# A planned float32 decoder layer: engine prices taken from the trace, the gates' strip loaded early, the residual stored by SyncE

## The chip, the cores and the metric

The kernel runs on one core of one Trainium2 chip. The metric is device microseconds of one execution. Engines: TensorE (PE), VectorE (DVE), ScalarE (ACT), GpSimd (POOL), and SyncE (SP), which only issues DMAs. ScalarE issues DMAs too, on a queue of its own; both queues are served by the core's 16 DMA engines.

## The reference, cut to what matters

One decoder layer for 256 tokens of 2048 features, all in float32:

```
sh1, sc1, g1, ..., g3 = split(silu(c) @ ada_w + ada_b, 9)
h = h + 0.5 * g1 * swiglu(modulate(rms_norm(h), sh1, sc1), ffn1 weights)
u = modulate(rms_norm(h), sh2, sc2)
p = u @ w_in            # q,k,v,z of DeltaNet; beta and decay gates (32 columns); q,k,v of attention; two merge gates
y_a = gated_delta_chunked(...)      # 16 heads, chunks of 64 tokens
y_b = moba_attention(...)           # 16 heads, causal, with a relative-position bias
h = h + g2 * ((sigmoid(gate_a) * (y_a @ w_proj_a) + sigmoid(gate_b) * (y_b @ w_proj_b)) @ w_out)
h = h + 0.5 * g3 * swiglu(modulate(rms_norm(h), sh3, sc3), ffn2 weights)
```

## The kernel before, in words

**Weights.** The dense products are cut into units, and a unit into steps of 128 rows (one k-tile) by 1024 columns of weights, 512 KB. A step's raw weights come by one or two DMAs on SyncE's queue into a ring of eight slots (`load_w`, L392 on; `fill`, `one_load`). `split` makes two fp32r parts of them: ScalarE casts to `wh`, VectorE subtracts to get `wl`. It runs LEAD = 3 steps ahead of TensorE, and VectorE's end of `wl` frees the ring slot. A step is then twelve matmuls of 512 columns (`mm`, L465): two token tiles, two column halves, three products (wh by the high part of x, wl by the high part, wh by the low part). There are 912 steps.

**Side work.** Everything else (norms, transposes, the DeltaNet and attention heads, the adaLN sections) is written as generators. `aside` puts one into a list with the time at which it can go on; `pump`, called once or twice a step, lets a generator run to its next `yield` if it is ready and if VectorE and ScalarE have room before the next weights are due. All of this happens while the program is written, so it fixes each engine's order of instructions. The times are those of `Clock`, an account that adds a price to an engine for every instruction issued through the wrappers V, S, PE, G (L184 is the wrapper's call, so all side work has this line). A generator is ready when what its last piece wrote is ready by the account (`clk.turn`), or at a time that it yields, such as `clk.PE + 8.0`. `late`, up to which side work may fill VectorE and ScalarE, counts the steps split ahead at W_STEP = 12 * W_MM each. `Clock.add` prices a DMA at 0.06 us of its engine plus DMA_LAG until it has landed.

**The mixer.** It follows the first FFN. `begin` in `mixer()` takes the residual `h` (eight pages of 128x512) out of use. At the mixer's step 8 (`KT // 2`) the hook `spill` stores all eight pages to DRAM (`hsp`) from ScalarE's queue and starts two generators, in this order:
- `late_params` loads the convolution weights and more, after 8 us zeroes two scratch arrays in DRAM (`xsc`, four stores of 256 KB), loads the tables of the position bias, and after 12 us stores the bias spread over 128 rows for each of 16 heads, 3 MB (`scr`), all from ScalarE's queue.
- `heads_params` loads the 128-column strip of w_in that holds the beta and decay gates, in two halves of 512 KB (rows of 512 bytes), from SyncE's queue (L956), each into a ring slot; 8 us after a half's issue ScalarE and VectorE split it in two parts. Then come 48 matmuls (16 k-tiles, three products each), the gates' arithmetic on small tiles, and a store of the cumulated decays (`gsc`).

Each DeltaNet group (four heads) later goes through DRAM several times: `dn_tile` loads a row of `gsc` and stores the matrix L to `lsc`; `dn_blocks` loads its diagonal blocks, inverts them, stores them into `xsc` and loads the whole matrices back (four loads of 256 KB) for TensorE. `dn_front` and `dn_back` use GpSimd's power. The units of the merge gates and the projections begin after `need_dn` and `need_mb`, which let all groups end. `reload_h` reads `hsp` back later.

Tiles of 128x512 come from a pool of 57 pages. `pump` holds a generator back when too few are free.

Of the kernel before, what the change touches and what calls it, by code (L numbers as in the profile page):

```python
# [13 lines left out]
F32 = mybir.dt.float32  # L14
# [29 lines left out]
OPEN = 8  # L44
FINISH = 3
BLOCKS = ((0, 4), (4, 8), (8, 12), (12, 16))
W_MM = 0.216
W_STEP = 12 * W_MM
W_H = 1.0
W_L = 1.2  # L50
RESERVE = 1.0
DMA_LAG = 2.6
AHEAD_LAST = 4.0
SPARE = 10
SPARE_ON = 3
HEADS_ON = 2
MB = 6
MB_MIX = 5
MARGIN = 0.0

CON = {}
_n = 0
# [48 lines left out]
    __slots__ = ("unit", "kt", "cols", "x", "first", "last", "load", "wh", "wl", "xs", "ready")  # L111


class Clock:

    def __init__(self):
        self.PE = self.ACT = self.DVE = self.POOL = 0.0
        self.after = self.turn = 0.0  # L120
        self.count = 0
        self.wrote, self.read = {}, {}
        self.spent = {"PE": 0.0, "ACT": 0.0, "DVE": 0.0, "POOL": 0.0}

    def begin(self):

# [2 lines left out]

    def seen(self, log, name, eng):  # L130
        t, by = log.get(name, (0.0, eng))
        return t + (0.05 if by == eng else 0.18)

    def free(self, name, eng):
        return max(self.seen(self.wrote, name, eng), self.seen(self.read, name, eng))
# [6 lines left out]
    def add(self, eng, op, args, kw):  # L142
        self.count += 1
        aps = [(k, a) for k, a in (*enumerate(args), *kw.items()) if isinstance(a, bass.AP)]
        outs = [a.tensor.name for k, a in aps if k in (0, "out", "accum_out")]
        ins = [a.tensor.name for k, a in aps if k not in (0, "out", "accum_out")]
        out = args[0] if args else kw["out"]
        n = 1
        for d in out.shape[1:]:
            n *= d  # L150
        lag = 0.0
        if op == "dma_start":
            cost, lag = 0.06, DMA_LAG
        elif eng == "PE":
            cost = 0.003 + n / 2400 * (1 if args[2].dtype == F32R else 2 if op == "transpose" else 4)
        elif eng == "DVE":
            cost = 0.065 + n / (960 if op in ("tensor_tensor", "tensor_sub", "tensor_add", "tensor_mul", "scalar_tensor_tensor") else 1500)
            if any(x.startswith("bk") for x in ins):
                cost = max(cost, 0.065 + n / 960) + 0.06
        elif eng == "ACT":  # L160
            cost = 0.1 + n / 1200
        else:
            cost = 0.9 + n / 30 if op == "tensor_tensor" else 0.1 + n / 290
        start = max([getattr(self, eng)] + [self.seen(self.wrote, x, eng) for x in ins] + [self.free(x, eng) for x in outs])
        end = start + cost
        setattr(self, eng, end)
        self.spent[eng] += cost
        for x in ins:
            self.read[x] = (end + lag, eng)
        for x in outs:  # L170
            self.wrote[x] = (end + lag, eng)
        self.after = end + lag + 0.18
        self.turn = max(self.turn, self.after)


# [22 lines left out]
def tile_hybrid_layer(ctx: ExitStack, tc: tile.TileContext, A, out, dbg=None):  # L198
# [5 lines left out]
    ctx.enter_context(tc.manual_schedule())  # L204

    clk = Clock()
    V, S, PE, G = (Timed(e, clk, n) for e, n in ((nc.vector, "DVE"), (nc.scalar, "ACT"), (nc.tensor, "PE"), (nc.gpsimd, "POOL")))
    serial = [0]
    held = []
    taken = [0]  # L210
# [60 lines left out]
    def ring_tile(shape):  # L271
        ring["out"] += 1
        return sb.tile(list(shape), F32, name=nm("ring"), tag="ring", bufs=RING)

    def ring_done():
        ring["out"] -= 1
# [212 lines left out]
    def aside(gen):  # L489
        side.append(Side(gen, clk.turn))  # L490
# [457 lines left out]

    def heads_params():

        parts = []
        for half in range(2):
            while ring["out"] >= RING:
                yield
            raw = ring_tile((P, 8, P))
            nc.sync.dma_start(raw, W_IN[half * 8 * P:(half + 1) * 8 * P, oB:oB + P].rearrange("(k p) n -> p k n", p=P))  # L956
            yield clk.PE + 8.0
            for n in range(2):
                wh, wl = page((P, 4, P), F32R), page((P, 4, P), F32R)
                S.copy(wh, raw[:, n * 4:n * 4 + 4, :])  # L960
                V.tensor_sub(wl, raw[:, n * 4:n * 4 + 4, :], wh.bitcast(F32))
                parts.append((wh, wl))
                if n:
                    ring_done()
                yield
        uh, ul = state["u"]
        b = sbank()
        for kt in range(KT):
            wh, wl = (w[:, kt % 4, :] for w in parts[kt // 4])
            PE.matmul(b[:, :T], wh, uh[:, kt, :], start=kt == 0, stop=False)  # L970
            PE.matmul(b[:, :T], wh, ul[:, kt, :], start=False, stop=False)
            PE.matmul(b[:, :T], wl, uh[:, kt, :], start=False, stop=kt == KT - 1)
        parts = None
        ba = page((2 * HEADS, T))
        V.tensor_copy(ba, b[:2 * HEADS, :T])
        yield
        b = sbank()
        for tt in range(NT):
            PE.transpose(b[:, tt * 32:tt * 32 + 32], ba[:, tt * P:(tt + 1) * P], ident[:32, :32])
        ab = small(64, "ab")  # L980
        V.tensor_copy(ab, b[:, :64])
        ab3 = ab.rearrange("p (t n) -> p t n", t=NT)
        W = NT * HEADS
        be = const(W, "beta")
        be3 = be.rearrange("p (t n) -> p t n", t=NT)
        S.activation(be3, ab3[:, :, 0:HEADS], AF.Tanh, scale=0.5)
        V.tensor_scalar(be, be, 0.5, 0.5, op0=ALU.mult, op1=ALU.add)
        yield
        x = small(W, "x")
        V.tensor_tensor(x.rearrange("p (t n) -> p t n", t=NT), ab3[:, :, HEADS:], dtb[:, None, :].to_broadcast([P, NT, HEADS]), op=ALU.add)  # L990
        e = small(W, "e")
        S.activation(e, x, AF.Abs)
        S.activation(e, e, AF.Exp, scale=-1.0)
        al = small(HEADS, "al")
        S.activation(al, alog, AF.Exp)
        yield
        z = small(W, "z")
        V.tensor_scalar(z, e, 2.0, None, op0=ALU.add)
        V.reciprocal(z, z)
        V.tensor_mul(z, z, e)  # L1000
        z2 = small(W, "z2")
        V.tensor_mul(z2, z, z)
        acc = small(W, "lp")
        V.tensor_scalar(acc, z2, 1.0 / 17, None, op0=ALU.mult)
        for k in range(7, 0, -1):
            V.scalar_tensor_tensor(acc, acc, 1.0 / (2 * k + 1), z2, op0=ALU.add, op1=ALU.mult)
        V.scalar_tensor_tensor(acc, acc, 1.0, z, op0=ALU.add, op1=ALU.mult)
        V.tensor_scalar(x, x, 0.0, None, op0=ALU.max)
        V.scalar_tensor_tensor(acc, acc, 2.0, x, op0=ALU.mult, op1=ALU.add)
        g = const(W, "g")  # L1010
        V.scalar_tensor_tensor(g.rearrange("p (t n) -> p t n", t=NT), acc.rearrange("p (t n) -> p t n", t=NT), -1.0,
                               al[:, None, :].to_broadcast([P, NT, HEADS]), op0=ALU.mult, op1=ALU.mult)
        yield
        b = sbank()
        for n, m in enumerate((C("tri"), bc(C("one0"), [P, P]), bc(C("one1"), [P, P]))):
            PE.matmul(b[:, n * W:(n + 1) * W], m, g, start=True, stop=True)
        gc = const(W, "gc")
        V.tensor_copy(gc, b[:, 0:W])
        ngc = const(W, "ngc")
        V.tensor_scalar(ngc, gc, -1.0, None, op0=ALU.mult)  # L1020
        rem = const(W, "rem")
        for n in range(2):
            r0 = n * 64
            V.tensor_sub(rem[r0:r0 + 64, :], b[r0:r0 + 64, (n + 1) * W:(n + 2) * W], gc[r0:r0 + 64, :])
        S.activation(rem, rem, AF.Exp)
        tot = const(2 * W, "tot")
        S.activation(tot, b[:, W:3 * W], AF.Exp)
        beg = const(W, "beg")
        S.activation(beg, gc, AF.Exp)
        V.tensor_mul(beg, beg, be)  # L1030
        beh = const(W, "beh")
        V.tensor_scalar(beh, be, 0.5, None, op0=ALU.mult)
        yield
        b = sbank()
        PE.transpose(b[:W, :P], gc, ident)
        gr = page((W, P))
        S.copy(gr, b[:W, :P])
        yield
        S.dma_start(gsc, gr)
        dn.update(be=be, beh=beh, gc=gc, ngc=ngc, rem=rem, tot=tot, beg=beg)  # L1040
# [516 lines left out]
    def mixer():  # L1557
        def begin():
            set_banks(MB_MIX)
            grow.pop(1)  # L1560
            held.clear()
            h, state["h"] = state["h"], None

            def spill():
                for tt in range(NT):
                    for n in range(4):
                        S.dma_start(hsp[:, tt, n * 512:(n + 1) * 512], h[tt][n])
                clk.turn = clk.PE
                aside(late_params())
                aside(heads_params())  # L1570
            hooks.setdefault(mix_at[0] + KT // 2, []).append(spill)

        mix_at = [nsteps[0]]
        ks = list(range(KT))
# [179 lines left out]
```

## Time and profile before, and how to read it

| | us |
|---|---|
| median of 3 runs | 2821.92 (2816.88 to 2828.46) |
| the profiled execution | 2811.26 |
| its span, first to last instruction | 2809.5 |
| mean granted TensorE clock | 0.995 of full speed |

The profile is of one execution. An engine's busy time is the union of its instructions. "a <- b" after an idle time names what ended the wait; a wait's list has total us, times, longest us. PEld is the weight load of TensorE. pg is any page, bk any PSUM bank.

### The profile page before, as it was taken

Reading aid. Unit: us, or ns where it says so; the run is one execution under the profiler, and the core shown is the slowest. Engines: PE = TensorE matmul, PEld = TensorE weight load, DVE = VectorE, ACT = ScalarE, POOL = GpSimd, SP = SyncE. Lnnn points to the kernel's source line nnn. Section 1 sums busy time; section 2 is a strip of 40 time slices with the busy share of each in tenths; the row PEclk is TensorE's granted clock in tenths of the full one; section 3 lists DMA queues with packets and bytes.
Section 4 is the critical chain, followed back from the end, with each engine's and each line's share of the span. In section 5 each row is a group of like instructions: output and inputs, shape, how many; then the busy total and the mean of one; then the engine's idle time right before and its main releaser. Section 6 shows DMA issues by size and latency. Waiting matters only on the chain.

```text
span 2809.5 us, 36472 instructions
## 1 busy us (share of the span) xinstructions
PE 2726.4 (97%) x12696; PEld 2256.8 (80%) x12696; DVE 2008.2 (71%) x2778; ACT 1386.9 (49%) x2166; POOL 47.1 (2%) x43
## 2 busy tenths in 40 slices
PE   5999999999998999999999999999999999999999
PEld 3888888888876888788888888888878888888887
DVE  6699788797954676867666899889656666544545
ACT  5534453444463564554645655455564444443443
POOL 0000000000000000000100000000000000000000
PEclk9999999999999999999999999999999999999999
DMA  9898659898968664646555998989557777656654
GB/s 333 278 314 280 215 184 358 278 354 303 337 204 204 188 180 138 175 124 171 159 156 164 317 284 283 327 300 337 185 160 240 245 241 247 210 190 194 194 187 135
DMA packets 321190, 658.34 MB, mean 234 GB/s; under 512 B 44815, under 2 KB 67938, under 8 KB 321006
## 3 DMA queue, kind: packets, MB, share of 16 engines
q1 hardware_dynamic: 282432, 634.97, 69.2%
q10 hardware_dynamic: 38574, 21.05, 3.2%
q8 instruction: 99, 1.62, 0.2%
q14 instruction: 85, 0.70, 0.1%
HBM read 644.86 MB, written 11.03 MB: 233 GB/s over the span
## 4 chain that ended last, share of the span: by engine, by line
PE 87%; DMA 5%; DVE 3%; ACT 3%; issue 1%; ACTq 0%; POOL 0%; SPq 0%; DVEq 0%; POOLq 0%
PE bk L465 81%; PE bk L184 6%; DMA ring<-in_w_in 2%; DVE pg L184 2%; ACT pg L184 1%; DVE wl L184 1%; DMA pg<-xsc 1%; ACT wh L184 1%; DMA ring<-in_ada_w 0%; ACT uh L184 0%; DMA pg<-in_x 0%; ACTq L184 0%; DMA xsc<-pg 0%; DMA ring<-in_w_proj_a 0%; DMA lsc<-pg 0%
## 5 line engine op out<-in xcount | busy, mean ns | idle before, releaser
L184 DVE TENSOR_TENSOR wl<-ring,wh 128x1024 fp32r<-128x1024 f32 x912 | 1112.9, 1223 | 597.7 <-ACT wh L184 583.4
L184 ACT CAST wh<-ring 128x1024 fp32r<-128x1024 f32 x912 | 959.9, 1055 | 972.6 <-PE bk L465 794.4
L465 PE MATMUL bk<-wh,uh 128*128 128x512 f32 x2560 | 1022.6, 399 | 3.4 <-ACT uh L184 2.6
L465 PE MATMUL bk<-wl,uh 128*128 128x512 f32 x2560 | 1001.3, 391 | 0.9 <-DVE wl L184 0.8
L465 PE MATMUL bk<-wh,ul 128*128 128x512 f32 x2560 | 853.5, 391 | 2.6 <-DVE ul L184 2.6
L465 PE MATMUL bk<-wh,pg 128*128 128x512 f32 x2176 | 719.1, 390 | 4.0 <-DVE pg L184 3.5
L465 PEld LDWEIGHTS bk<-wh,ul 128*128 128x128 f32 x2560 | 482.1, 188 | 109.4 <-DVE ul L184 6.3
L465 PEld LDWEIGHTS bk<-wh,uh 128*128 128x128 f32 x2560 | 483.1, 189 | 99.4 <-ACT uh L184 4.2
L465 PEld LDWEIGHTS bk<-wl,uh 128*128 128x128 f32 x2560 | 483.5, 189 | 94.9 <-DVE wl L184 2.2
L465 PEld LDWEIGHTS bk<-wh,pg 128*128 128x128 f32 x2176 | 408.5, 188 | 91.5 <-DVE pg L184 5.4
L465 PE MATMUL bk<-wl,pg 128*128 128x512 f32 x1088 | 423.6, 389 | 0.0
L184 DVE SCALAR_TENSOR_TENSOR pg<-ring,csil,pg 128x512 f32<-128x512 f32 x552 | 388.5, 746 | 8.2 <-DMA ring<-in_ada_w 8.2
L465 PEld LDWEIGHTS bk<-wl,pg 128*128 128x128 f32 x1088 | 204.3, 188 | 42.2
L184 ACT COPY pg<-bk 128x512 f32<-128x512 f32 (+3 forms) x201 | 108.6, 563 | 183.7 <-PE bk L184 108.5
L184 DVE TENSOR_TENSOR pg<-bk,pg 128x512 f32<-128x512 f32 (+3 forms) x225 | 148.6, 677 | 46.4 <-PE bk L465 38.4
L184 DVE TENSOR_TENSOR pg<-pg,pg 128x256 fp32r<-128x256 f32 (+11 forms) x388 | 159.3, 415 | 6.0 <-ACT pg L184 0.9
L184 PE MATMUL bk<-con,pg 128*128 128x128 f32 (+2 forms) x775 | 118.4, 277 | 42.2 <-DVE pg L184 17.4
L184 PEld LDWEIGHTS bk<-con,pg 128*128 128x128 f32 (+2 forms) x775 | 95.8, 142 | 68.4 <-DVE pg L184 17.1
L184 PEld LDWEIGHTS bk<-pg,pg 128*128 128x128 f32 (+2 forms) x834 | 111.3, 192 | 26.3 <-issue 15.2
L184 PE MATMUL bk<-pg,pg 128*128 128x128 f32 (+3 forms) x834 | 118.7, 287 | 12.5 <-DMA pg<-xsc 10.3
L184 ACT ACTIVATE pg<-pg 128x128 f32<-128x128 f32 (+1 forms) x176 | 78.6, 451 | 50.9 <-DVE pg L184 29.1
L184 ACT ACTIVATE pg<-bk 128x128 f32<-128x128 f32 (+1 forms) x136 | 60.0, 451 | 78.9 <-PE bk L465 45.0
(110 smaller groups left out, 679.3 us busy)
## 6 DMA issues: line engine op xcount, KB each, us to landing
ring<-in_ffn_w SPq DMA_DIRECT2D x704, 256.0 KB, 4.1
ring<-in_ada_w SPq DMA_DIRECT2D x288, 512.0 KB, 5.4
ring<-in_w_in SPq DMA_DIRECT2D x512, 256.0 KB, 4.2
ring<-in_ffn_w SPq DMA_DIRECT2D x176, 512.0 KB, 4.6
ring<-in_w_in SPq DMA_DIRECT2D x34, 512.0 KB, 4.7
ring<-in_w_proj_a SPq DMA_DIRECT2D x64, 256.0 KB, 5.2
ring<-in_w_proj_b SPq DMA_DIRECT2D x64, 256.0 KB, 5.9
ring<-in_w_out SPq DMA_DIRECT2D x32, 512.0 KB, 4.3
```

The costliest lines, as they stand in the source:

```text
L184: r = f(*args, **kw)
L465: nc.tensor.matmul(st.unit.banks[tt, c], xs[i == 2][:, tt * P:(tt + 1) * P], w[:, c * 512:(c + 1) * 512], start=st.first and i == 0, stop= ...
```

## The change

Three edits.

- The account's prices and rules are replaced: the matmul of 512 columns from 0.216 to 0.2268 us, DMA issue from 0.06 to 0.4, DMA landing from 2.6 to 5.0, GpSimd's power from 0.9 + n/30 to 0.35 + 0.17 n, extra price for per-partition scalar operands, for accumulating outputs and for reductions, semaphore delays between engines from 0.18 to 0.13 or 0.2 us; a generator must now be ready 0.3 us (MARGIN) before TensorE's time. SyncE gets a wrapper, SY.
- `heads_params` issues the strip as four loads of 256 KB into four pages at mixer step 4, waits 32 us (HEADS_WAIT) on the account's clock, then splits the four parts as before.
- The eight pages of the residual are stored from SyncE's queue, one at each of the mixer's steps 4 to 11; `late_params` starts at step 9.

```diff
-W_MM = 0.216
+W_MM = 0.2268
-DMA_LAG = 2.6
+DMA_LAG = 5.0
+DMA_ISSUE = 0.4
-MARGIN = 0.0
+MARGIN = 0.3
+HEADS_WAIT = 32.0
...
     def seen(self, log, name, eng):
         t, by = log.get(name, (0.0, eng))
-        return t + (0.05 if by == eng else 0.18)
+        return t + ((0.0 if eng == "PE" else 0.05) if by == eng else 0.2 if by == "PE" else 0.13)
...
+        ps = any(x.startswith("bk") for x in ins)
+        each = sum(size(a) == 1 for k, a in aps if k not in (0, "out", "accum_out")) if n > 1 else 0
         lag = 0.0
         if op == "dma_start":
-            cost, lag = 0.06, DMA_LAG
+            cost, lag = DMA_ISSUE, DMA_LAG
         elif eng == "PE":
-            cost = 0.003 + n / 2400 * (1 if args[2].dtype == F32R else 2 if op == "transpose" else 4)
+            cost = 0.003 + n / 2400 * 2 if op == "transpose" else 0.0135 + n / 2400 if args[2].dtype == F32R else 0.008 + n / 2400 * 4
         elif eng == "DVE":
-            cost = 0.065 + n / (960 if op in ("tensor_tensor", "tensor_sub", "tensor_add", "tensor_mul", "scalar_tensor_tensor") else 1500)
-            if any(x.startswith("bk") for x in ins):
-                cost = max(cost, 0.065 + n / 960) + 0.06
+            if op == "tensor_reduce":
+                n = size(args[1])
+            two = op in ("tensor_tensor", "tensor_sub", "tensor_add", "tensor_mul", "scalar_tensor_tensor", "tensor_reduce")
+            cost = 0.068 + 0.06 * each + n / (960 if two or ps else 1900)
         elif eng == "ACT":
-            cost = 0.1 + n / 1200
+            cost = (0.055 if ps else 0.1) + 0.09 * (each + ("accum_out" in kw)) + n / 1200
         else:
-            cost = 0.9 + n / 30 if op == "tensor_tensor" else 0.1 + n / 290
-        start = max([getattr(self, eng)] + [self.seen(self.wrote, x, eng) for x in ins] + [self.free(x, eng) for x in outs])
+            cost = 0.35 + 0.17 * n if op == "tensor_tensor" else 0.12 + n / 1000
+        start = max([getattr(self, eng)] + [self.seen(self.wrote, x, eng) for x in ins]
+                    + [self.seen(self.read, x, eng) if op == "dma_start" else self.free(x, eng) for x in outs])
...
-        self.after = end + lag + 0.18
+        self.after = end + lag + 0.2
...
     def heads_params():
 
+        raws = [page((P, 4, P)) for _ in range(4)]
+        for n in range(4):
+            SY.dma_start(raws[n], W_IN[n * 4 * P:(n + 1) * 4 * P, oB:oB + P].rearrange("(k p) n -> p k n", p=P))
+        yield clk.PE + HEADS_WAIT
         parts = []
-        for half in range(2):
-            while ring["out"] >= RING:
-                yield
-            raw = ring_tile((P, 8, P))
-            nc.sync.dma_start(raw, W_IN[half * 8 * P:(half + 1) * 8 * P, oB:oB + P].rearrange("(k p) n -> p k n", p=P))
-            yield clk.PE + 8.0
-            for n in range(2):
-                wh, wl = page((P, 4, P), F32R), page((P, 4, P), F32R)
-                S.copy(wh, raw[:, n * 4:n * 4 + 4, :])
-                V.tensor_sub(wl, raw[:, n * 4:n * 4 + 4, :], wh.bitcast(F32))
-                parts.append((wh, wl))
-                if n:
-                    ring_done()
-                yield
+        for n in range(4):
+            wh, wl = page((P, 4, P), F32R), page((P, 4, P), F32R)
+            S.copy(wh, raws[n])
+            V.tensor_sub(wl, raws[n], wh.bitcast(F32))
+            parts.append((wh, wl))
+            raws[n] = None
+            yield
...
-            def spill():
-                for tt in range(NT):
-                    for n in range(4):
-                        S.dma_start(hsp[:, tt, n * 512:(n + 1) * 512], h[tt][n])
-                clk.turn = clk.PE
-                aside(late_params())
-                aside(heads_params())
-            hooks.setdefault(mix_at[0] + KT // 2, []).append(spill)
+            def spill(n):
+                SY.dma_start(hsp[:, n // 4, n % 4 * 512:(n % 4 + 1) * 512], h[n // 4][n % 4])
+                h[n // 4][n % 4] = None
+            for n in range(8):
+                hooks.setdefault(mix_at[0] + 4 + n, []).append(lambda n=n: spill(n))
+
+            def params(gen):
+                clk.turn = clk.PE
+                aside(gen())
+            for n, gen in ((4, heads_params), (KT // 2 + 1, late_params)):
+                hooks.setdefault(mix_at[0] + n, []).append(lambda gen=gen: params(gen))
```

## Rows read from the trace of the kernel before

**Rows 1.** The page: span, TensorE's busy time, the DMA packets.
```profile
span 2809.5 us, 36472 instructions
...
PE 2726.4 (97%) x12696; PEld 2256.8 (80%) x12696; DVE 2008.2 (71%) x2778; ACT 1386.9 (49%) x2166; POOL 47.1 (2%) x43
...
DMA packets 321190, 658.34 MB, mean 234 GB/s; under 512 B 44815, under 2 KB 67938, under 8 KB 321006
```
**Rows 2.** Windows: us, busy time (instructions) of each engine, clock, DMA share, GB/s.
```profile
0.00:100.00 100.00, 65.30 (x272) 52.74 (x273) 69.26 (x96) 52.81 (x88) 1.65 (x7) 1.00 0.94 331
...
1000.00:1600.00 600.00, 582.64 (x3064) 490.74 (x3063) 425.70 (x806) 327.94 (x717) 34.32 (x19) 0.99 0.60 172
```
**Rows 3.** Waits of TensorE, 780 to 912 us: total, times, longest.
```profile
PE bk L184 <- ACT pg L184: 13.3, 2, 11.2
...
PE bk L465 <- DVE wl L184: 0.8, 1, 0.8
PE bk L465 <- ACT wh L184: 0.6, 1, 0.6
```
**Rows 4.** Waits of TensorE, 912 to 2060 us.
```profile
PE bk L184 <- DMA pg<-xsc: 10.3, 6, 2.7
PE bk L184 <- DVE pg L184: 6.3, 7, 1.6
PE bk L465 <- DVE pg L184: 3.5, 4, 1.9
```
**Rows 5.** Timeline, 857 to 886 us: start us, us, engine, instruction [idle before].
```profile
857.92 0.67 ACTq L184 DMA_DIRECT2D scr<-pg  x1
...
858.58 0.38 SPq L956 DMA_DIRECT2D ring<-in_w_in  x1
...
884.44 0.62 ACT L184 CAST pg<-ring 128x512 fp32r<-128x512 f32 x1 [19.10 <-DMA ring<-in_w_in]
...
885.12 0.58 PE L184 MATMUL bk<-uh,pg 128*128 128x256 f32 x1 [11.24 <-ACT pg L184]
```
**Rows 6.** DMA queues, 862 to 884 us: packets, MB, share of 16 engines.
```profile
q10 hardware_dynamic: 1422, 2.18, 87.1%
q1 hardware_dynamic: 1287, 0.99, 13.4%
```
**Rows 7.** Windows of two stretches at half clock.
```profile
877.44:891.09 13.65, 5.97 (x25) 5.70 (x26) 3.81 (x5) 3.03 (x4) 0.00 (x0) 0.50 1.00 191
1082.24:1085.65 3.41, 3.41 (x12) 2.93 (x12) 2.20 (x3) 0.00 (x0) 0.00 (x0) 0.50 0.00 1
```
**Rows 8.** Timeline at the spill.
```profile
814.99 0.40 ACTq L184 DMA_DIRECT2D hsp<-pg  x1
...
825.23 1.99 ACT L184 CAST wh<-ring 128x1024 fp32r<-128x1024 f32 x2 [5.46 <-DMA hsp<-pg]
```
**Rows 9.** SyncE's own waits, 770 to 910 us.
```profile
SPq L402 <- DVE wl L184: 54.9, 23, 10.8
```
**Rows 10.** The chain of waits: start us, us, what.
```profile
129.06 81.64 PE bk L465 x360
```
**Rows 11.** DMA issues: count, KB each, median us to landing.
```profile
pg<-xsc ACTq DMA_DIRECT2D x16, 256.0 KB, 5.8
```
**Rows 12.** Timeline, a DeltaNet group's loads and TensorE's wait for them.
```profile
1071.70 2.07 ACTq L184 DMA_DIRECT2D pg<-xsc  x4
...
1081.78 1.63 PE L184 MATMUL bk<-pg,pg 128*128 128x128 f32 x8 [2.09 <-DMA pg<-xsc]
```
**Rows 13.** Groups of instructions by form: busy us, mean ns, then idle before.
```profile
L184 DVE SCALAR_TENSOR_TENSOR pg<-ring,csil,pg 128x512 f32<-128x512 f32 x552 | 388.5, 746 | 8.2 <-DMA ring<-in_ada_w 8.2
...
L184 POOL TENSOR_TENSOR rkq<-ssq,mhalf 128x16 f32<-128x16 f32 x4 | 12.6, 3142 | 424.7 <-DVE ssq L184 412.9 <-DVE st L184 11.8
```
**Rows 14.** Two tiles' instructions: duration ns min/median/max, first and last start us.
```profile
L184 DVE SCALAR_TENSOR_TENSOR pg<-pg,sa,pg x32: 343/347/353, 1135.5 to 1503.2; 128x128 f32<-128x128 f32 x32
...
L402 SPq DMA_DIRECT2D ring<-in_w_proj_a x64: 328/424/1053, 1580.9 to 1770.1; - x64
```

More of the change, by code (lines that the diff above doesn't have):

```diff
@@ L111, with size @@
     __slots__ = ("unit", "kt", "cols", "x", "first", "last", "load", "wh", "wl", "xs", "ready")
+def size(ap):
+    n = 1
+    for d in ap.shape[1:]:
+        n *= d
+    return n
 class Clock:
     def __init__(self):
-        self.PE = self.ACT = self.DVE = self.POOL = 0.0
+        self.PE = self.ACT = self.DVE = self.POOL = self.SP = 0.0
         self.after = self.turn = 0.0
@@ L122, in __init__ @@
         self.wrote, self.read = {}, {}
-        self.spent = {"PE": 0.0, "ACT": 0.0, "DVE": 0.0, "POOL": 0.0}
+        self.spent = {"PE": 0.0, "ACT": 0.0, "DVE": 0.0, "POOL": 0.0, "SP": 0.0}
     def begin(self):
@@ L147, in add @@
         out = args[0] if args else kw["out"]
-        n = 1
-        for d in out.shape[1:]:
-            n *= d
+        n = size(out)
+        ps = any(x.startswith("bk") for x in ins)
+        each = sum(size(a) == 1 for k, a in aps if k not in (0, "out", "accum_out")) if n > 1 else 0
         lag = 0.0
         if op == "dma_start":
-            cost, lag = 0.06, DMA_LAG
+            cost, lag = DMA_ISSUE, DMA_LAG
         elif eng == "PE":
-            cost = 0.003 + n / 2400 * (1 if args[2].dtype == F32R else 2 if op == "transpose" else 4)
+            cost = 0.003 + n / 2400 * 2 if op == "transpose" else 0.0135 + n / 2400 if args[2].dtype == F32R else 0.008 + n / 2400 * 4
         elif eng == "DVE":
-            cost = 0.065 + n / (960 if op in ("tensor_tensor", "tensor_sub", "tensor_add", "tensor_mul", "scalar_tensor_tensor") else 1500)
-            if any(x.startswith("bk") for x in ins):
-                cost = max(cost, 0.065 + n / 960) + 0.06
+            if op == "tensor_reduce":
+                n = size(args[1])
+            two = op in ("tensor_tensor", "tensor_sub", "tensor_add", "tensor_mul", "scalar_tensor_tensor", "tensor_reduce")
+            cost = 0.068 + 0.06 * each + n / (960 if two or ps else 1900)
         elif eng == "ACT":
-            cost = 0.1 + n / 1200
+            cost = (0.055 if ps else 0.1) + 0.09 * (each + ("accum_out" in kw)) + n / 1200
         else:
-            cost = 0.9 + n / 30 if op == "tensor_tensor" else 0.1 + n / 290
-        start = max([getattr(self, eng)] + [self.seen(self.wrote, x, eng) for x in ins] + [self.free(x, eng) for x in outs])
+            cost = 0.35 + 0.17 * n if op == "tensor_tensor" else 0.12 + n / 1000
+        start = max([getattr(self, eng)] + [self.seen(self.wrote, x, eng) for x in ins]
+                    + [self.seen(self.read, x, eng) if op == "dma_start" else self.free(x, eng) for x in outs])
         end = start + cost
@@ L206, in tile_hybrid_layer @@
     clk = Clock()
-    V, S, PE, G = (Timed(e, clk, n) for e, n in ((nc.vector, "DVE"), (nc.scalar, "ACT"), (nc.tensor, "PE"), (nc.gpsimd, "POOL")))
+    V, S, PE, G, SY = (Timed(e, clk, n) for e, n in ((nc.vector, "DVE"), (nc.scalar, "ACT"), (nc.tensor, "PE"), (nc.gpsimd, "POOL"), (nc.sync, "SP")))
     serial = [0]
```

## The prediction

> **What bounds the kernel now.** I read the page first. TensorE is busy 97% of the span, 2726.4 of 2809.5 us [rows 1], and its work isn't changed: every matmul and transpose stands in both versions. So the change can only act on the 83.1 us in which TensorE is idle, and on what a slowed TensorE clock costs. The windows then say where the idle time lies: 34.7 us of it in the first 100 us [rows 2], which no edit reaches, since the opening is issued in a fixed order. Of the rest I asked the waits of TensorE, stretch by stretch. Between 60 and 780 us the list is empty. From 780 to 912 us one wait stands out, 11.2 us on ScalarE [rows 3]. From 912 to 2060 us there are seventeen short ones, 20.1 us in all, none over 2.7 us [rows 4]. After that come only the hand-written passage into the last FFN and the final stores, both as they were.
>
> The timeline shows what the long wait is. The store of the attention's bias table (scr, 3 MB) is issued at 857.92; 0.66 us later SyncE issues the second half of the gates' strip of w_in. ScalarE's cast of it can't begin before 884.44, after 19.10 us of idle, and TensorE, having come to the gates' matmuls, stands still for 11.24 us [rows 5]. The two queues' packets say why: from 862 to 884 us the ACT queue (the store) holds 87.1% of the DMA engines' time, and SP's queue is let through one packet for one, 1287 against 1422, mostly packets of 512 B from the strip [rows 6]. The idle stretch also costs clock: from 877.44 to 891.09 us the granted clock is 0.50 (1.2 instead of 2.4 GHz), with 5.97 us of TensorE work in it [rows 7]. Work at half clock takes twice as long, so 2.98 us are lost. **The strip's price is 11.24 + 2.98 = 14.2 us.**
>
> **The strip.** The change issues it as four loads of 256 KB into pages at mixer step 4, and turns to it 32 us later on the account's clock. Step 4 lies near 800 us, since the hook of step 8 ran at 815 us, where the spill begins [rows 8], and a step is 2.72 us and some side work; so the strip is asked for some 40 us before the store of scr can be issued (the work that ends in this store is now started one step later, but no longer behind the spill). Its 1 MB, at the 331 GB/s that the DMA engines moved in the first 100 us [rows 2], is 3 us; landing by 815 us and use near 832 us leave room. Casts and subtractions are as many as before, in pages instead of ring slots; four more pages are held for some 35 us, in a stretch in which no group of the mixer is open yet. I take the whole 14.2 us; the bounds are 0 (the wait only changes its cause) and 14.2.
>
> **The spill.** Eight stores on ScalarE's queue, the first at 814.99; the weights' cast behind them comes 5.46 us late [rows 8], and TensorE waits 0.8 us for wl and 0.6 us for wh [rows 3]: 1.4 us. On SyncE each store goes out alone behind a step's two weight loads. What covers it: SyncE waited 54.9 us of 770 to 910 us for a ring slot to be freed by VectorE [rows 9], so some 0.4 us of issue a step is free; eight slots of the ring, one a step, are 22 us of cover for a late load. If that cover went, the eight issues would cost 8 x 0.4 = 3 us. I take -1.4 us; bounds -1.4 and +3.
>
> **The account.** It decides when a piece of side work is given to the engines; it issues nothing itself. Its step was 12 x 0.216 = 2.59 us and becomes 12 x 0.2268 = 2.72; the chain shows 81.64 us for 360 matmuls, 0.2268 each [rows 10], so the new figure is what this chip did. A DMA was held to be ready 0.06 + 2.6 + 0.18 = 2.84 us after its turn to issue; now 0.4 + 5.0 + 0.2, and with the margin of 0.3 it is 5.9. The loads of xsc landed in 5.8 us [rows 11]: issued from 1071.70 on, awaited by TensorE until 1081.78 [rows 12]. The shift of 3.06 us is more than the longest of these six waits (2.7), which hold 10.3 us [rows 4]. Two of them also fell to half clock with 3.41 us of work each; one row stands for both [rows 7]: 2 x 1.7 = 3.4 us. Bounds for this part: 0 and 13.7. I take 11.7, near the upper end, because the shift exceeds each wait; 2 us are left for a ScalarE queue that issues the loads later than the account thinks.
> The other eleven waits (6.3 + 3.5 us [rows 4]) are for VectorE running behind the account. VectorE's multiply-add with a per-partition scalar was 0.598 us and is 0.661, against 0.746 measured; GpSimd's power of 16 columns was 1.43 us and is 3.07, against 3.142 [rows 13]. Half of the gap closes, so I take half, 5 us; bounds 0 and 9.8. Against this a new plan puts the pieces elsewhere and meets new waits: I take 4 us, about four of the present mean of 1.2 us (20.1 / 17); bounds 0 and 20.1, a plan as bad as the present one.
>
> **Sum:** 14.2 + 1.4 + 11.7 + 5 - 4 = 28 us. The profiled execution took 2811.3 us; the median of the runs is 2821.9, 0.4% above it. The forecast goes from the median: 2822 - 28 = 2794 us, 1.0% faster. The measurement of this kernel tells about 0.5%, 14 us, from no change; the strip alone is just that.
>
> **Rivals.**
> 1. *The plan gives nothing.* New waits eat all that the account's new figures save; only 14.2 + 1.4 stay: 2806 us. For it: such plans move everything behind the first changed piece. Against it: six of the waits have one cause, and its figure moves by more than they last. 0.18, half of it on either side of 0.5%.
> 2. *The store of scr now starves the weights.* With packets let through one for one, SP's queue got 1287 in 22 us [rows 6]; at 2 KB a packet that is 120 GB/s, where a step's 512 KB in 2.72 us want 193. The store's 3.1 MB last 32 us (2.18 MB in 22 us), so the weights fall behind by 73 x 32 = 2.3 MB, 4.5 ring slots of eight. A full ring covers that; one at half doesn't, and a wait like today's returns: 2794 + 14 = 2808. 0.09.
> 3. *Loads late behind the stores.* Steps 4 to 11 want 512 + 256 KB each and the strip 1 MB, 7.3 MB in 8 x 2.72 = 22 us, 335 GB/s on one queue, where 331 is the most of a whole stretch [rows 2]; if the queue gives the mean of 234 [rows 1], the last load is 10 us late: 2794 + 10 = 2804. The ring's 22 us speak against it. 0.04. The Trainium skill (Perfetto Trace Analysis, DMA Optimizations) advises one engine for inputs and another for outputs, and this change does the opposite; by it this rival's 2804 would be the result. No row here shows SP's queue carrying both, and ScalarE's stall on the separate queue [rows 8] speaks the other way.
> 4. *VectorE overfilled, slower.* A step of 2.72 us lets the account give VectorE 0.13 us more a step, while its prices are still under the measured ones (0.661 against 0.746). If VectorE can't do it, each weight's wl comes late by that: at most 1060 / 2.72 = 390 steps between 1000 and 2060 us x 0.13 = 51 us, 2845 us. It decides where VectorE's busy share nears 100%. Against it: 425.70 of 600 us from 1000 to 1600 [rows 2]; and the higher prices of its own work take back about as much. 0.08.
> 5. *It doesn't do what it says.* The 32 us are counted on the account's clock, from the moment at which the pump takes the piece up; if that is late, the strip meets the store again and its 14.2 us stay: 2794 + 14 = 2808. 0.05.
> Longer waits could also push the DeltaNet chains past the barrier of the projections; the last of their scalings ran at 1503.2 us and the projections' first load at 1580.9 [rows 14], 78 us of slack. Five DMAs in a row x 3.06 = 15 us a group, 61 us if all four groups stood in one line: no chance of its own.
>
> **The numbers.** Forecast 0.56, rivals 0.18, 0.09, 0.04, 0.08, 0.05. Faster by over 0.5%: 0.56 + 0.09 + a fifth or so of rivals 2 and 3 = 0.69. Slower: 0.08. Within: 0.23. The range: below, nearly all that the waits hold, 14.2 + 1.4 + 13.7 + 9.8 = 39 us, and some 9 us of spread (the runs shown lie 11.6 us apart): 2774; above, rivals 1, 2, 3 and 5 with the runs' spread, 2818; rival 4 is left out. The forecast's own range is 2780 to 2804.
>
> **What would show it.** Right: in 780 to 912 us no wait on the strip and no half clock after 860; the loads of the strip near 800 us, stores of hsp by SyncE with no idle of ScalarE behind them; TensorE's waits on xsc under 3 us in sum; idle time of TensorE near 55 us. Wrong: waits of wh for ring loads between 840 and 890 us (rivals 2 and 3), many waits of matmuls for wl after 1000 us (rival 4), a sum of waits from 912 to 2060 us that stays near 20 us (rival 1).

## The result, and the profile after

The kernel after takes 2786.39 us (median of 4 runs, 2784.27 to 2790.01) against 2821.61 us (2816.88 to 2828.46) for the kernel before, measured beside it: a ratio of 0.9879, 95% interval 0.9858 to 0.99. It is 35 us faster, 1.2%; forecast were 28 us, and a range that holds the result. The profiled execution after took 2785.33 us, its granted clock was 0.997.

The page of after, its span and its engines' line [rows 1]:

```profile
span 2783.5 us, 36476 instructions
...
PE 2720.1 (98%) x12696; PEld 2252.2 (81%) x12696; DVE 2007.5 (72%) x2778; ACT 1387.1 (50%) x2166; POOL 47.3 (2%) x43
```

TensorE is idle for 63.4 us instead of 83.1. The waits of TensorE after, from 780 to 912 us [rows 3]; as before, total us, times, longest us:

```profile
PE bk L477 <- ACT pg L196: 3.2, 1, 3.2
PE bk L196 <- ACT pg L196: 2.0, 1, 2.0
PE bk L477 <- ACT uh L196: 1.4, 2, 0.8
PE bk L477 <- DVE ul L196: 1.1, 2, 0.8
PE bk L477 <- DVE wl L196: 0.8, 1, 0.8
```

The 11.2 us on ScalarE are gone; a new wait of 3.2 us stands at the top (below). The same view from 912 to 2000 us, where the passage into the last FFN hasn't begun yet (in before it begins 26 us later, so [rows 4] go to 2060):

```profile
PE bk L477 <- DVE pg L196: 3.5, 4, 1.9
PE bk L196 <- DVE pg L196: 3.0, 4, 1.3
PE bk L196 <- DMA pg<-xsc: 2.1, 4, 1.2
PE bk L477 <- ACT pg L196: 0.2, 1, 0.2
```

The waits on xsc fell from 10.3 to 2.1 us, VectorE's from 6.3 + 3.5 to 3.0 + 3.5. At half clock [rows 7] the windows show in this range:

```profile
787.09:797.33 10.24, 8.72 (x21) 6.04 (x22) 3.52 (x6) 6.27 (x14) 0.55 (x1) 0.50 0.35 102
845.12:848.53 3.41, 3.41 (x9) 2.65 (x8) 2.32 (x3) 3.41 (x6) 0.00 (x0) 0.50 0.53 150
```

The first lies in the passage into the mixer, where before has some too (a mean of 0.77 from 787 to 798 us); the second follows the new wait. One more of 3.41 us comes at 2039.78.

The two profiles lie only 26 us apart, since the profiled execution of before was one of its shortest. So the kernel before was profiled once more:

> The kernel before once more, for a second profile: its runs lie 14 us apart and the first profile was of a short one. Theory (the wait for the strip varies with the two queues): the wait at the gates' matmuls is longer than 11.2 us by as much as this run is longer than 2811 us. Rival: that wait is the same within 1 us, and the runs differ in the waits on xsc, in half clock or in the opening.

That execution took 2823.7 us, span 2821.9. Its timeline (start, duration, engine, operation; in brackets the idle time before it) and its window at half clock, which answer to [rows 5, 7]:

```profile
855.55 0.67 ACTq L184 DMA_DIRECT2D scr<-pg  x1
856.62 0.38 SPq L956 DMA_DIRECT2D ring<-in_w_in  x1
...
887.76 0.62 ACT L184 CAST pg<-ring 128x512 fp32r<-128x512 f32 x1 [24.79 <-DMA ring<-in_w_in]
888.44 0.58 PE L184 MATMUL bk<-uh,pg 128*128 128x256 f32 x1 [16.93 <-ACT pg L184]
```

```profile
874.45:894.93 20.48, 6.49 (x27) 6.08 (x28) 4.07 (x5) 3.03 (x4) 0.00 (x0) 0.50 0.95 191
```

The same wait costs 16.93 us of idle and 6.49 / 2 = 3.2 us of clock here: 20 us, against 14.2 in the execution that the prediction was worked from. The store of scr was 0.66 us ahead of the strip's second half there, 1.07 us here. The theory is only half right: of the 12.4 us between the two spans this wait makes 5.7. Half clock makes 7.5, of which 0.3 stand at the strip and 4.0 at the waits on xsc: these lasted about as long (10.3 and 11.4 us in sum), but the half clock at them covers 6.82 us of TensorE work in the first profile and 14.82 in the second.

The table splits each profile. "Half clock" is TensorE's busy time in the windows granted 0.50, halved; the idle columns are TensorE's, by stretch. All times in us.

| kernel | median, ratio | span | idle 780-912 | idle 912-2000 | half clock |
|---|---|---|---|---|---|
| before, first profile | 2821.6 | 2809.5 | 17.8 | 19.9 | 10.8 |
| before_again | 2823.7 (one run) | 2821.9 | 23.0 | 21.0 | 18.3 |
| after | 2786.4, 0.9879 | 2783.5 | 9.2 | 8.8 | 7.6 |
| e1_account | 2790.3, 0.9891 | 2787.7 | 10.5 | 11.2 | 9.5 |
| e2_strip | 2804.5, 0.9940 | 2802.4 | 8.1 | 19.6 | 15.5 |
| e3_spill | 2802.7, 0.9938 | 2801.8 | 7.0 | 22.0 | 11.2 |
| e4_strip_spill | 2806.1, 0.9945 | 2806.3 | 6.9 | 25.0 | 13.2 |
| e5_old_dma_price | 2804.3, 0.9936 | 2803.4 | 8.9 | 20.2 | 15.1 |
| e6_late_sp | 2783.3, 0.9865 | 2785.3 | 6.0 | 13.6 | 7.3 |
| e7_spaced | 2809.7, 0.9959 | 2805.3 | 5.6 | 24.9 | 14.6 |
| e10_strip_behind_8 | 2798.7, 0.9925 | 2797.3 | 17.2 | 10.5 | 12.7 |
| e11_strip_behind_32 | 2824.3, 1.0012 | 2817.8 | 13.7 | 23.6 | 24.5 |
| e12_pages_54 | 2826.7, 1.0023 | 2825.1 | 8.9 | 35.6 | 21.0 |
| e13_late_sp_lag6 | 2788.9, 0.9892 | 2786.4 | 6.6 | 13.1 | 9.1 |

Against before_again, which lies near the median, the sum closes within 2 us: the span is 38.4 us shorter, of which 13.8 are idle time from 780 to 912 us, 12.2 idle time from 912 to 2000 us and 10.7 half clock, 36.7 in sum.

### The profile page after: what moved, and what is told of

Same layout as the page of the kernel before. It is cut to its first block, busy times and chain, and to the rows that moved or that the text cites. A ratio compares the mean times of both kernels' runs of the same rounds, so it can differ in the third digit from the quotient of the medians.

```text
span 2783.5 us, 36476 instructions
## 1 busy us (share of the span) xinstructions
PE 2720.1 (98%) x12696; PEld 2252.2 (81%) x12696; DVE 2007.5 (72%) x2778; ACT 1387.1 (50%) x2166; POOL 47.3 (2%) x43
## 4 chain that ended last, share of the span: by engine, by line
PE 88%; DMA 4%; ACT 3%; DVE 3%; issue 1%; ACTq 0%; SPq 0%; DVEq 0%
PE bk L477 82%; PE bk L196 6%; DVE pg L196 2%; ACT pg L196 2%; DMA pg<-xsc 1%; ACT wh L196 1%; DVE wl L196 1%; DMA ring<-in_w_in 1%; DMA ring<-in_ada_w 0%; ACT uh L196 0%; DMA pg<-in_x 0%; ACTq L196 0%; DMA xsc<-pg 0%; DMA hsp<-pg 0%; DMA ring<-in_ffn_w 0%
## 5 line engine op out<-in xcount | busy, mean ns | idle before, releaser
L196 ACT COPY pg<-bk 128x512 f32<-128x512 f32 (+4 forms) x201 | 108.6, 567 | 172.5 <-PE bk L196 87.7
L196 ACT ACTIVATE pg<-bk 128x512 f32<-128x512 f32 (+1 forms) x136 | 59.9, 460 | 79.1 <-PE bk L477 48.5
```

The costliest lines, as they stand in the source:

```text
L196: r = f(*args, **kw)
```

## The experiments

Each edit alone came first: the account's, the strip's, the spill's, and the last two together.

**The account alone** (e1; strip and spill as before, both at step 8).

```diff
-            raws = [page((P, 4, P)) for _ in range(4)]
+            raw = ring_tile((P, 8, P))
+            nc.sync.dma_start(raw, W_IN[half * 8 * P:(half + 1) * 8 * P, oB:oB + P].rearrange("(k p) n -> p k n", p=P))
...
+                        S.dma_start(hsp[:, tt, n * 512:(n + 1) * 512], h[tt][n])
```

> The new account alone; the strip is loaded in two halves into ring slots and the spill goes out from ScalarE, as before the change. Theory (each part saves its own waits): the waits of TensorE from 912 us on fall to under 11 us, on xsc to about 2 us, as after the change; the long wait for the strip near 870 to 885 us stays with 10 us or more and its stretch at half clock. The time lies 12 to 20 us under the kernel before, near 2805 us. Rival (the account only moves waits about): the waits from 912 us on stay near 20 us and the time is that of the kernel before within 6 us.

It took 2790.3 us, 0.9891 (0.9868 to 0.9914), 32 us faster. The theory that the strip's wait would stay fell. The timeline of this kernel, the strip's second half and the store:

```profile
841.36 0.38 SPq L968 DMA_DIRECT2D ring<-in_w_in  x1
...
857.92 0.67 ACTq L196 DMA_DIRECT2D scr<-pg  x1
```

Under the new plan the second half goes out 16.6 us ahead of the store instead of 0.66 us behind it, and the wait isn't there. The account alone comes within 4 us of the whole change, and the intervals overlap: that the other two edits add anything to it isn't shown.

**The strip alone** (e2; four early loads into pages, from step 4) and **the spill alone** (e3; a page a step on SyncE, the strip as before).

```diff
+            hooks.setdefault(mix_at[0] + 4, []).append(early)      # e2: early() starts heads_params
...
+                SY.dma_start(hsp[:, n // 4, n % 4 * 512:(n % 4 + 1) * 512], h[n // 4][n % 4])      # e3
```

> The early strip alone: the four loads into pages at mixer step 4 with the 32 us of waiting; the old account; the spill goes out from ScalarE at step 8 with late_params behind it, as before. Theory: no wait of TensorE over 4 us between 800 and 912 us, the waits from 912 us on stay near 20 us; 14 us are saved, 2807 us. Rival (the store of scr starves the weights instead): waits for wh or wl of 5 us and more between 860 and 900 us; 2815 us or more.

> The spill alone: one page a step from SyncE at steps 4 to 11; the strip in two halves into ring slots after step 8, the old account. Theory: the waits of 1.3 us at 826 us go, the wait for the strip stays at 10 us or more; 2820 us, not to be told from before. Rival (ScalarE's held-up queue was what brought the strip and the store of scr together): the wait for the strip shrinks under 6 us, 2812 us.

The strip alone gave 0.994 (0.992 to 0.996), 17.7 us; the spill alone 0.9938 (0.9915 to 0.9961), 19.4 us, where 1.4 were forecast for it. The timeline of the spill alone:

```profile
846.29 0.38 SPq L957 DMA_DIRECT2D ring<-in_w_in  x1
...
847.89 0.66 ACTq L185 DMA_DIRECT2D scr<-pg  x1
```

With the eight stores off ScalarE's queue the rest moves a little, the strip goes out 1.6 us ahead of the store instead of behind it, and the same wait is gone. What the spill "gave" is the strip's wait.

**Strip and spill, with the old account (e4).**

```diff
-DMA_LAG = 5.0
-DMA_ISSUE = 0.4
+DMA_LAG = 2.6
...
-            cost = 0.35 + 0.17 * n if op == "tensor_tensor" else 0.12 + n / 1000
+            cost = 0.9 + n / 30 if op == "tensor_tensor" else 0.1 + n / 290
```

> Strip and spill as after the change, with the old account. Theory: no wait over 4 us from 800 to 912 us, waits from 912 us on near 20 us; 15 us saved, near 2806 us. With the account alone the savings add up to the whole change's 35 us within 8 us. Rival (the parts need each other): the two savings add up to less than 25 us, or this kernel has a new wait of over 5 us between 830 and 900 us.

16.1 us (0.9945, 0.9925 to 0.9965). The halves don't add up to the whole: 31.9 + 16.1 = 48 against 35.2. So the strip's wait was removed by each of the three edits, and counted in each.

**The meeting, brought back (e10, e11).** If the order of two issues is what matters, the strip put right behind the store of scr must bring the wait back under the new account, and a longer wait of the generator must hide it again. HEADS_WAIT is 8 in the first and 32 in the second.

```diff
         S.dma_start(scr, bv[:, None, :].to_broadcast([HEADS, P, 3 * P]))
+        clk.turn = clk.PE
+        aside(heads_params())
...
-            for n, gen in ((4, heads_params), (KT // 2 + 1, late_params)):
+            for n, gen in ((KT // 2 + 1, late_params),):
```

> The changed kernel with heads_params started right behind the store of scr and 8 us of waiting instead of 32: the strip's four loads stand behind the store, as its second half did before the change. Theory (the wait before the change was the strip meeting the store, and the account turning to it too soon): ScalarE's cast waits for the strip and TensorE stands still for 10 us or more at the gates' matmuls, with a stretch at half clock; 2800 us or more. Rival (the collision alone is harmless, the ring slots held by the strip did it): no wait of TensorE over 4 us between 850 and 920 us; under 2792 us.

> As the kernel before this one, with the 32 us of waiting: the strip still meets the store, but is turned to later. Theory: the strip lands in 25 to 35 us, so the wait of TensorE at the gates' matmuls shrinks under 5 us and the time is within 6 us of the changed kernel, 2786 to 2792 us. Rival (what counts is that the loads stand ahead of the store): a wait of 10 us or more stays; 2800 us.

With 8 us (e10) it takes 2798.7 us, 12 more than after. Its timeline:

```profile
853.48 0.67 ACTq L196 DMA_DIRECT2D scr<-pg  x1
...
860.43 18.21 SPq L196 DMA_DIRECT2D pg<-in_w_in  x4
...
883.07 0.62 ACT L196 CAST pg<-pg 128x512 fp32r<-128x512 f32 x1 [17.71 <-DMA pg<-in_w_in]
884.68 0.79 PE L479 MATMUL bk<-wh,uh 128*128 128x512 f32 x1 [9.54 <-ACT wh L196]
```

Four issues take SyncE 18.21 us, ScalarE stands 17.71 us at the strip's cast, and TensorE 9.54 us, here at the next weights: their cast is queued behind the strip's on ScalarE. So the wait takes two things: the meeting, and a turn to the strip that comes too soon (e1 and e3 also turn to it 8 us after an issue, without the meeting, and don't wait). With 32 us (e11) no wait on the strip is left, yet the time is 2824.3 us. The meeting costs there too, by another way:

```profile
860.50 18.56 SPq L196 DMA_DIRECT2D pg<-in_w_in  x4
879.15 14.12 SPq L416 DMA_DIRECT2D ring<-in_w_in  x11
...
890.61 1.04 ACT L196 CAST wh<-ring 128x1024 fp32r<-128x1024 f32 x1 [14.07 <-DMA ring<-in_w_in]
...
891.71 0.79 PE L479 MATMUL bk<-wh,uh 128*128 128x512 f32 x1 [5.85 <-ACT wh L196]
```

The strip's four issues hold SyncE for 18.56 us, the next weights are asked for only at 879.15, and TensorE waits 5.85 us for them, with 5.94 us of work at half clock from 887.88 to 898.12: 8.8 us, and the stall that rival 2 named. The greater part of the loss lies later and is taken up under the pages.

**The DMA's price (e5).** After, with this price alone as it was.

```diff
-DMA_LAG = 5.0
-DMA_ISSUE = 0.4
+DMA_LAG = 2.6
+DMA_ISSUE = 0.06
```

> The changed kernel with the old two prices of a DMA (0.06 us of issue, 2.6 us to landing), all else as changed. Theory (the DMA price removed the waits on xsc): TensorE's waits on xsc are back at 7 to 13 us from 2.1, with one or two stretches at half clock; no long wait between 800 and 912 us; 2795 to 2800 us. Rival (the step's length, 2.72 instead of 2.59, and the margin did it): the waits on xsc stay under 4 us; 2784 to 2790 us.

2804.3 us, 0.9936 (0.9915 to 0.9958): half of the gain is gone, 18 us. The waits of TensorE from 912 to 2000 us, the xsc row:

```profile
PE bk L196 <- DMA pg<-xsc: 14.6, 7, 4.8
```

14.6 us against 2.1 after, and three stretches at half clock at these waits (from 1070, 1190 and 1429 us, 11.0 us of TensorE work, 5.5 us lost) where after has none: 18 of the 20 us by which the spans differ.

**The new wait at 844.80 (e6, e13).** The timeline of after:

```profile
834.35 4.57 ACTq L196 DMA_DIRECT2D xsc<-pg  x4
...
842.78 0.32 ACTq L196 DMA_DIRECT2D pg<-in_rel_bias  x1
843.22 1.04 ACT L196 CAST wh<-ring 128x1024 fp32r<-128x1024 f32 x1 [9.56 <-DMA pg<-in_k_past]
...
844.80 0.55 PE L477 MATMUL bk<-wh,uh 128*128 128x512 f32 x1 [3.17 <-ACT pg L196]
```

`late_params` has ScalarE issue seven DMAs from 834.35 on (k_hot and k_past at 840.85 and 841.23 among them). The next cast stands behind them and begins after 9.56 us without work; TensorE stands 3.17 us, and 3.41 us run at half clock. The test: those seven by SyncE.

```diff
-                S.dma_start(heads_view(t, n), v3(zero))
+                SY.dma_start(heads_view(t, n), v3(zero))
...
-        S.dma_start(hot, A["k_hot"])
+        SY.dma_start(hot, A["k_hot"])
```

> The changed kernel with the four zeroing stores and the three small table loads of late_params issued by SyncE instead of ScalarE. Theory (ScalarE's issue of these seven, 9.56 us of idle before its next cast, makes TensorE's new wait of 3.2 us at 845 us): that wait and its 3.41 us at half clock go, 4.9 us less, 2781 to 2783 us. Rival (on SyncE they hold up the weight loads, which the store of scr then starves): waits for wh or wl of over 3 us between 840 and 900 us, 2786 us or more.

The wait and its half clock are gone (idle 9.2 to 6.0 us), but the plan behind it is another, with 5.6 us on xsc, and 4.8 us more idle from 912 to 2000 us. 2783.3 us, 0.9865 (0.9846 to 0.9884), is the lowest median of all, yet its interval overlaps that of after; a gain isn't shown. A longer landing time was added to that version to take away the waits on xsc:

```diff
-DMA_LAG = 5.0
+DMA_LAG = 6.0
```

> The changed kernel with the zeroing stores and table loads issued by SyncE, as in the kernel that did that alone, and 6.0 us to a DMA's landing instead of 5.0. Theory (the account is still 1 us short for the loads of xsc): TensorE's waits on xsc fall under 2 us in sum from 5.6, no other wait grows, 2778 to 2782 us. Rival (each microsecond of waiting holds pages longer and moves the plan): the waits from 912 us on stay at 13 us or more and the time is 2784 us or more.

2788.9 us, as the rival had it. Its waits from 912 to 2000 us no longer list xsc; these came instead:

```profile
PE bk L196 <- DVE pg L196: 4.9, 3, 1.9
PE bk L196 <- ACT pg L196: 4.4, 2, 4.1
PE bk L477 <- DVE pg L196: 3.5, 4, 1.9
```

**The store and the weights (rival 2; e7).** From 858 to 884 us the queues and the weight loads of after [rows 6], and SyncE's issues in the timeline:

```profile
q10 hardware_dynamic: 1694, 2.60, 83.3%
q1 hardware_dynamic: 576, 1.05, 10.6%
...
ring<-in_w_in SPq DMA_DIRECT2D x6, 256.0 KB, 17.8
```

```profile
857.53 25.31 SPq L414 DMA_DIRECT2D ring<-in_w_in  x7
```

SP's queue moved 1.05 MB in 26 us, 40 GB/s, a third of the 120 that the prediction gave it. A load landed 17.8 us after its issue (the median), and seven issues took 25.31 us, the first of them 0.33 and each other 3.5 to 4.3. The full ring just covered it: 0.8 us of wait on wl is all that came of it. The test of this was to spread the stores: the zeroing 8 us apart, scr in eight pieces 12 us apart.

```diff
+                yield clk.PE + 8.0
...
-        S.dma_start(scr, bv[:, None, :].to_broadcast([HEADS, P, 3 * P]))
+        for r in range(8):
+            S.dma_start(scr[:, r * 16:(r + 1) * 16, :], bv[:, None, :].to_broadcast([HEADS, 16, 3 * P]))
+            yield clk.PE + 12.0
```

> The changed kernel with the zeroing stores of late_params one by one, 8 us apart, and the store of scr in eight pieces of 16 rows, 12 us apart, all from ScalarE as before. Theory (a long DMA on ScalarE's queue keeps SP's queue from its descriptors): the 3.2 us wait at 845 us and the 0.8 us wait for wl at 892 us go, no weights' cast waits over 3 us for the ring between 840 and 1000 us; 2780 to 2783 us. Rival (the same DMA work in more pieces only holds ScalarE up more often): TensorE's waits between 800 and 1000 us add up to 9 us or more as now; 2786 us or more.

Here the theory was half right. From 780 to 912 us TensorE is idle only 5.6 us, the least of all. But the kernel takes 2809.7 us. The last scaling of the DeltaNet chains and the projections' first load [rows 14], in after and then in this kernel (durations, then first and last start):

```profile
L196 DVE SCALAR_TENSOR_TENSOR pg<-pg,sa,pg x32: 344/347/352, 1144.4 to 1499.3; 128x128 f32<-128x128 f32 x32
...
L414 SPq DMA_DIRECT2D ring<-in_w_proj_a x64: 328/424/1036, 1555.0 to 1744.8; - x64
```

```profile
L196 DVE SCALAR_TENSOR_TENSOR pg<-pg,sa,pg x32: 343/347/353, 1137.7 to 1579.1; 128x128 f32<-128x128 f32 x32
...
L417 SPq DMA_DIRECT2D ring<-in_w_proj_a x64: 328/424/1140, 1533.9 to 1763.7; - x64
```

The chains begin 7 us earlier and end 80 us later, behind the first load of what has to wait for them. e11 shows the same: its last scaling is at 1590.5 us, its projections' first load at 1545.4. The projections can't go on before these chains end: of e7's 24.9 us of waits from 912 to 2000 us, 13.7 lie between 1540 and 1650, for pages of VectorE and ScalarE.

**The pages (e12).** Both versions hold pages for longer around 900 us (e7 the bias' page up to the last piece of scr at 984 us; e11 the strip's, whose gates' matmuls come at 912 to 918 us instead of 859 to 865). If the pool is what stretches the chains, after with a smaller pool must do the same with every issue where it was.

```diff
-PAGES = 57
+PAGES = 54
```

> The changed kernel with a pool of 54 pages instead of 57, nothing else. Theory (two earlier kernels lost 20 us and more because pieces of the last DeltaNet group were refused pages and ran into the barrier of the projections): the last scaling of DeltaNet comes after the projections' first load, as in those two, TensorE has waits of over 5 us in sum between 1500 and 1640 us with stretches at half clock, and the time is 2800 us or more. Rival (those kernels lost their time on ScalarE's and SyncE's queues, not on pages): the last scaling stays near 1500 us, 2784 to 2792 us.

2826.7 us, 1.0023 (1.0006 to 1.0041): three pages fewer take back the whole gain. Its waits from 912 to 2000 us and its chains' last scaling:

```profile
PE bk L196 <- DVE pg L196: 21.3, 12, 5.3
```

```profile
L196 DVE SCALAR_TENSOR_TENSOR pg<-pg,sa,pg x32: 342/347/353, 1140.5 to 1578.8; 128x128 f32<-128x128 f32 x32
...
L414 SPq DMA_DIRECT2D ring<-in_w_proj_a x64: 328/424/625, 1530.8 to 1757.6; - x64
```

Want of pages alone gives the same picture: chains that end at 1578.8 us, the first load at 1530.8, 21.3 us of waits for VectorE's pages instead of 3.0. From 1540 to 1650 us TensorE is idle for 14.4 us, in e7 for 14.0, in after for 0.2; another 11.2 us come from 1760 to 1830 us, and those e7 doesn't have (0.6). That want of pages is also what happened in e7 and e11 is the likely reading, not a shown one: neither was run with a larger pool. Pages needn't be all of it either: in e13, with 57 pages and a longer landing time alone against e6, the last scaling moved from 1498.2 to 1551.9 us, 6 us ahead of the projections' first load.

## Why the prediction was right, and where it was not

1. **The strip.** The wait went as forecast, to nothing. Its size was taken from one execution: 14.2 us there, 20 in the other. The step that was mis-sized is "I take the whole 14.2 us", with 14.2 as the upper bound: a wait that comes of two issues about a microsecond apart had a size of its own in each of the two executions, and it should have had a bound on the upper side. By before_again the strip was worth 6 us more than taken and the waits on xsc with their clock 5 more (point 4); spill, VectorE and new waits together came out 3 lower. In sum that is about the 7 us between the forecast 28 and the measured 35. The forecast's own words hold the reason: it took the change from a profile 10 us below the median and then set it against the median.
2. **What removes it.** The prediction put it down to the early load. e1, e2 and e3 show that each of the three edits alone removes it, e10 that the order of the two issues brings it back. The size that the prediction gave the strip belongs to the wait, not to the edit, and the sum held because all three edits were made together.
3. **The spill.** As forecast: the first store of hsp was issued by SyncE at 809.8, the issues took 0.43 us in the median, the longest 1.26, and no wait of TensorE followed; the 1.4 us are within what these profiles can tell. Rival 3 isn't there. The Trainium skill (Perfetto Trace Analysis, DMA Optimizations) says that it may make sense to give inputs and outputs an issuing engine each. Here the mixed queue cost nothing that shows: SyncE's waits for ring slots from 770 to 910 us are 54.1 us, 54.9 before [rows 9], and e3, whose edit is this mix, has no wait of TensorE over 0.8 us for a weight from 780 to 912 us.
4. **The price of a DMA.** Forecast 11.7 us. e5 gives 12.5 us of waits and 5.5 of half clock; between the first profile of before and that of after the waits fell by 8.2, from before_again by 9.3, with 7.4 us of clock at them (14.82 / 2), 16.7 us together. The mechanism held; mis-sized was the clock, counted at 3.4 us from one execution.
5. **VectorE's waits.** 9.8 us became 6.5, a gain of 3.3 where 5 were taken. In e5, with the old price of a DMA, they are 5.9 us, so the gain doesn't hang on that price; which of the other new figures brought it no run separates.
6. **New waits.** 4 us were taken, about four of 1.2 us in the new plan. What came is mainly one: 3.17 us behind ScalarE's seven issues, and 1.7 of clock. The amount was near, the place wasn't named: the prediction didn't count these issues. That `late_params` begins a step later isn't the reason: e1, where it begins at step 8 as before, has the wait too, 3.8 us, and e4, with the later start and the old account, has none over 0.8 us there. It came with the new account's plan. In before the same seven (from 843.30 on) kept ScalarE's cast 4.83 us, and TensorE didn't wait; in after they kept it 9.56 us.
7. **Rival 2** was nearer than its 0.09. "One packet for one" was read from a stretch in which SP's queue was full of packets of the strip. Where SyncE had to issue against the store, it got 576 packets beside 1694. The Trainium skill (DMA: Bandwidth & Descriptors, Queues, rings and completion order) says that each DMA engine takes turns between queues it has work for; the rows of before agree in packets (1287 beside 1422). In before_again it is 951 beside 1441 in the same 22 us behind the store. This and the rows of after don't speak against it, if SyncE's slow issues (some 4 us each in after) left its queue with little work, which no run shows. The ring's eight slots, which the prediction named as cover, held: 17.8 us of landing against 22 us of slots. In e11, where the strip's issues stood behind the store too, they didn't hold: TensorE waited 5.85 us for weights.
8. **The chains past the barrier** were given "no chance of its own", for 78 us of slack. e7, e11 and e12 ended them 45 to 48 us beyond the projections' first load. The slack was counted in DMA time alone; the chains' length hangs on pages too, and three pages are worth all of the change. In after this didn't happen, so the sum held. It was the rival that could have turned the sign, and it was left out of the list.
9. **Rivals 1, 4 and 5** weren't seen: the waits from 912 us to the passage into the last FFN fell by more than half (from 20.6 to 8.8 us), VectorE's busy time from 1000 to 1600 us is 442.75 of 600 us, and the strip met nothing. TensorE's idle time came out at 63.4 us where the prediction's last part said near 55. That figure was a slip: it is 83.1 - 28, but 6.4 of the 28 us (2.98 + 3.4) are clock and no idle time, so its own sum gives 61.

## What to carry to other kernels

Before an edit is credited with a wait, look at what makes that wait: where it is the order of two issues about a microsecond apart, any edit ahead of them can remove it or bring it, its size differs by execution, and the parts of a change don't add up. A planner that decides when work is issued should have its DMA price from the trace; the few microseconds it was short were worth half of this change. And the slack of side work isn't its distance to the barrier alone: it is also what the shared buffers allow, so a change that holds buffers longer is to be priced there.

## What the runs showed of the hardware

- A DMA issue on SyncE took 0.43 us in a quiet stretch and 3.5 to 5.4 us (after from 857.9 us, e10 from 860.4) while ScalarE's queue carried the 3 MB store; the weights' loads in after then landed after 17.8 us. The cost of the meeting lies in the issue as well as in the transfer.
- The same seven DMA issues kept ScalarE from its next cast for 4.83 us in before and for 9.56 us in after; the four stores that zero xsc took 2.81 us to issue there, 4.57 us here.
- Short waits can be paid twice: 3.17 us of idle were followed by 3.41 us at half clock (1.2 GHz), and around the end of the 16.93 us stood 20.48 us of it. It isn't so each time: behind the wait on xsc near 1310 us the clock stayed full after 2.7 us of idle in the first profile of before, and fell after 2.4 us in before_again.
